# The last four heads' values by products of 512 columns, and one more gate behind the last head's attention

## The chip, the core and the metric

The kernel runs on one core of a Trainium2 chip. The metric is device time in microseconds of one execution. Before the change three executions took 2167.63 to 2169.94 us, median 2169.21.

## What is computed

One layer of a hybrid decoder trunk on 512 tokens of width 2048, in float32: a root-mean-square norm, an input projection, three kinds of mixers side by side, an output projection added to the input, and a squared-ReLU MLP. The change touches the projections of two of the mixers.

```python
h = rmsnorm(x, norm1_w)
proj = h @ w_in
sb_q, sb_k, sb_v, sc_b, sc_c, sc_h, gdn_qkv, gdn_z, gdn_a, gdn_b = jnp.split(proj, cuts, axis=-1)
y_sb = stick_breaking_attention(heads(sb_q), heads(sb_k), heads(sb_v))      # 6 heads of 128
y_sc = sc_b * causal_depthwise_conv(sc_c * sc_h, sc_conv_w)                 # 4 groups of 128
y_gdn = gdn_mixer(gdn_qkv, gdn_z, gdn_a, gdn_b, ...)                        # 6 heads, ends with * silu(gdn_z)
x = x + jnp.concatenate([y_sb, y_sc, y_gdn], axis=-1) @ w_out
```

In the stick-breaking attention the weights of a row come from the scores by a softplus, a cumulative sum along the keys and an exponential. sb_v has six heads of 128 columns. The delta-rule mixer (gdn) multiplies its normed output with silu(gdn_z), head by head; that is the gate.

## The kernel before

Products are made as three products of numbers split into a high part (fp32r) and the remainder: `mm3` (L114 to L118) multiplies high with high (L116), high with low (L117) and low with high (L118). All of them run on TensorE (PE). The activations of the layer's input are split once and kept for the whole mixer part: `xw`, 16 tiles `big` of 128 inputs by 512 tokens. Weights are read as needed by `wload` (L97): a DMA of 128 x 512 into `raw` on SyncE's queue (SP), a cast into `whi` on ScalarE (ACT, L103) and a subtraction into `wlo` on VectorE (DVE, L104). Each of `raw`, `whi` and `wlo` has four buffers. `gemm` (L129) makes one product of 128 output columns for all 512 tokens out of four such loads: 16 input tiles times three matmuls, 48 in all, with the weights as the stationary side and 512 tokens moving. It accumulates in a PSUM tile `mm`, of which there are three (MMB).

The mixers are called in the order of the calls L665 to L713, but a scheduler of the language orders the instructions of each engine, by the order of the program, by raised priorities (`base` and `scan` have 2000, weight loads 400) and by its own idea of when each is ready. The order on each engine is then fixed in the program: each engine runs its list strictly one after the other and waits where an operand is not ready.

The delta-rule heads come first. `gdn_scan` (L496) goes through four blocks of 128 tokens in steps, each a few small matmuls with an operation of ACT or DVE between them: L507, the bias on DVE (L509), L512, a copy on ACT (L514), L517, the state on DVE (L522), and the output (L526, L530, L532, L533). Behind the last block follow a square on ACT (L537), a sum on DVE (L539), a reciprocal root on ACT (L146, L148), a scaling on DVE (L541), four transposes on PE (L544) and a copy on ACT (L546). `gdn_gate(h)` (L549) is one `gemm` and a silu, and multiplies the head's output. `sc_group` (L561) makes three such products for one group of the short convolution; its third product stays in its `mm` tile until the convolution has been made on DVE (L573 to L576).

When the last scan is done, its memory is handed to the attention's pool `sbp` (L696). `sb_qk(h)` (L590) makes a head's query and key by `gemm` and splits them (`sb_split`, L580). `sb_attn(h)` (L593) makes the scores `z` on PE, then a chain on DVE and ACT (L608 to L625, with a cumulative sum L622), transposes the weights on PE (L633), splits them (L637, L638) and multiplies them with the values (L646 to L650).

The values of heads 0 and 1 are made at the kernel's start and come back by `v_load`. Those of heads 2 and 3 and of 4 and 5 are made by `v_stage(1)` and `v_stage(2)` (L269): for each of 16 input tiles and each of four blocks of 128 tokens three matmuls (L279, L280, L281) with the tokens as the stationary side and 256 columns of the weight moving, into the four halves of two `mm` tiles. One weight load of 512 columns holds two input tiles. `v_evac` (L231) scales and splits them into `vhl` (with a plain copy of the last block in `v3`).

Behind the attention the output projection starts: `gemm(wo[m], yh)`, where `yh` are the mixers' outputs, split at L733 and L734 and taken in the order `ORDER`, whose last entries are delta-rule head 3, attention head 4, delta-rule head 4, attention head 5 and delta-rule head 5.

Of the kernel before, what the change touches and what calls it, by code (L numbers as in the profile page):

```python
# [11 lines left out]
F32 = mybir.dt.float32  # L12
F32R = mybir.dt.float32r
AF = mybir.ActivationFunctionType
ALU = mybir.AluOpType

P = 128
T = 512
NB = T // P
D = 2048  # L20
KT = D // P
# [33 lines left out]
def trunk(ctx, tc, xT, wv1, wv2, wa, wo, wu, wd, vec, wf, out, dbg=None):  # L55
    nc = tc.nc
    V, S, G, PE = nc.vector, nc.scalar, nc.gpsimd, nc.tensor
# [15 lines left out]
    def mmps():  # L73
        pool, bufs = pool_of_mm
        return pool.tile([P, 512], F32, name="mm", tag="mm", bufs=bufs)

    def xps(tag):
        pool, bufs = pool_of[tag]
        return pool.tile([P, 512], F32, name=tag, tag=tag, bufs=bufs)
# [8 lines left out]
    def tmp(n=512):  # L88
        return per.tile([P, n], F32, name="tmp", tag="tmp", bufs=4)
# [7 lines left out]
    def wload(src, n, prio=None):  # L97
        with tc.high_priority(WPRIO if prio is None else prio):
            raw = per.tile([P, 512], F32, name="raw", tag="raw", bufs=4)
            nc.sync.dma_start(out=raw[:, :n], in_=src)  # L100
            hi = per.tile([P, 512], F32R, name="whi", tag="whi", bufs=4, align_bytes=256)
            lo = per.tile([P, 512], F32R, name="wlo", tag="wlo", bufs=4, align_bytes=256)
            S.copy(out=hi[:, :n], in_=raw[:, :n])  # L103
            V.tensor_tensor(out=lo[:, :n], in0=raw[:, :n], in1=hi[:, :n].bitcast(F32), op=ALU.subtract)  # L104
        return hi, lo
# [23 lines left out]
    def gemm(src, acts):  # L129
        p = mmps()  # L130
        for c in range(KT // CHUNK_KT):
            gemm_chunk(p, src, acts, c)
        return p

    def silu(x, s):

        S.activation(out=s, in_=x, func=AF.Abs)
        S.activation(out=s, in_=s, func=AF.Exp, scale=-1.0)
        S.activation(out=s, in_=s, func=AF.Ln, bias=1.0)
        V.scalar_tensor_tensor(out=s, in0=x, scalar=0.0, in1=s, op0=ALU.min, op1=ALU.subtract)  # L140
        S.activation(out=s, in_=s, func=AF.Exp)
        V.tensor_tensor(out=x, in0=x, in1=s, op=ALU.mult)
# [27 lines left out]
    def pt(shape, name, tag=None, bufs=1, dt=F32):  # L170
        return ph_pool.tile(shape, dt, name=name, tag=tag or name, bufs=bufs)
# [14 lines left out]
    xw = []  # L186
# [7 lines left out]
    for k in range(KT):  # L194
        hi, lo = wload(wv1[:, k, :], 268, 0)
# [6 lines left out]
                               op0=ALU.mult, op1=ALU.subtract)  # L202
        for b in range(NB):
            s = slice(b * P, (b + 1) * P)
# [15 lines left out]
    p = xps("r")  # L220
    PE.matmul(p, lhsT=ones, rhs=acc, start=True, stop=True)
    rsqrt_exp(R, p, 1.0 / D, None)
    rtok = pt([P, NB], "rtok")
    p = xps("r")
# [3 lines left out]
    rtoks = pt([P, NB], "rtoks")  # L228
    S.mul(out=rtoks, in_=rtok, mul=SCALE)

    def v_evac(src_of_blk, pool):  # L231

        hl = pool.tile([P, 2, NB, 256], F32R, name="vhl", bufs=2)
        v3 = pool.tile([P, 256], F32, name="v3", bufs=2)
        for b in range(NB):
            src = src_of_blk(b)
            S.activation(out=hl[:, 0, b], in_=src, func=AF.Copy, scale=rtok[:, b:b + 1])
            V.scalar_tensor_tensor(out=hl[:, 1, b], in0=src, scalar=rtok[:, b:b + 1],
                                   in1=hl[:, 0, b].bitcast(F32), op0=ALU.mult, op1=ALU.subtract)
            if b == NB - 1:  # L240
                S.activation(out=v3, in_=src, func=AF.Copy, scale=rtok[:, b:b + 1])
        return hl, v3

    vt = [None] * 3
    ab = pt([P, NB, 12], "ab")
# [3 lines left out]
    for c in range(2):  # L249
        t = tmp()  # L250
        for b in (2 * c, 2 * c + 1):
            S.activation(out=t[:, (b % 2) * 256:(b % 2) * 256 + 256], in_=v1p[b][:, :256], func=AF.Copy,
                         scale=rtok[:, b:b + 1])
        nc.sync.dma_start(out=vd[:, 2 * c:2 * c + 2].rearrange("p b f -> p (b f)"), in_=t)

    def v_load():
        hl = sp_pool.tile([P, 2, NB, 256], F32R, name="vhl", bufs=2)
        v3 = sp_pool.tile([P, 256], F32, name="v3", bufs=2)
        for c in range(2):
            t = tmp()  # L260
            nc.sync.dma_start(out=t, in_=vd[:, 2 * c:2 * c + 2].rearrange("p b f -> p (b f)"))
            o = hl[:, :, 2 * c:2 * c + 2].rearrange("p w b f -> p w (b f)")
            S.copy(out=o[:, 0], in_=t)
            V.tensor_tensor(out=o[:, 1], in0=t, in1=o[:, 0].bitcast(F32), op=ALU.subtract)
            if c == 1:
                S.copy(out=v3, in_=t[:, 256:512])
        vt[0] = (hl, v3)

    def v_stage(i):  # L269
        pp = [mmps(), mmps()]  # L270
        for c in range(0, KT, 2):
            hi, lo = wload(wv2[i - 1][:, c:c + 2, :].rearrange("p k f -> p (k f)"), 512)
            for kk in range(2):
                k = c + kk
                ws = slice(kk * 256, kk * 256 + 256)
                for b in range(NB):
                    s = slice(b * P, (b + 1) * P)
                    o = pp[b // 2][:, (b % 2) * 256:(b % 2) * 256 + 256]
                    PE.matmul(o, lhsT=xw[k][:, 0, s], rhs=hi[:, ws], start=k == 0 and b % 2 == 0, stop=False)  # L279
                    PE.matmul(o, lhsT=xw[k][:, 0, s], rhs=lo[:, ws], start=False, stop=False)  # L280
                    PE.matmul(o, lhsT=xw[k][:, 1, s], rhs=hi[:, ws], start=False, stop=k == KT - 1 and b % 2 == 1)  # L281
        vt[i] = v_evac(lambda b: pp[b // 2][:, (b % 2) * 256:(b % 2) * 256 + 256], sp_pool)

    ys = [None] * KT

# [29 lines left out]
    p = xps("r")  # L315
# [233 lines left out]
    def gdn_gate(h):  # L549
        p = gemm(wa[18 + h], xw)  # L550
        z = tmp()
        V.tensor_tensor(out=z, in0=p, in1=R, op=ALU.mult)
        silu(z, tmp())
        y = ys[10 + h]
        V.tensor_tensor(out=y, in0=y, in1=z, op=ALU.mult)
# [24 lines left out]
    def sb_split(p, name):  # L580
        hl = sp_pool.tile([P, 2, 512], F32R, name=name, tag=name, bufs=2)
        S.copy(out=hl[:, 0], in_=p)
        V.tensor_tensor(out=hl[:, 1], in0=p, in1=hl[:, 0].bitcast(F32), op=ALU.subtract)
        l0 = sp_pool.tile([P, P], F32, name=name + "0", tag=name + "0", bufs=2)
        S.copy(out=l0, in_=p[:, 0:P])
        return hl, l0

# [2 lines left out]
    def sb_qk(h):  # L590
        qk[h] = sb_split(gemm(wa[24 + 2 * h], xw), "sq") + sb_split(gemm(wa[24 + 2 * h + 1], xw), "sk")
# [93 lines left out]
    base(5)  # L685
    gdn_gate(3)
    sc_group(1)
    gdn_gate(4)
    sc_group(2)
    sc_group(3)  # L690
    scan(5)
# [5 lines left out]
    sp_pool = sbp.__enter__()  # L697
    sb_qk(0)
    v_load()
    sb_attn(0)  # L700
    sb_qk(1)
    sb_attn(1)
    v_stage(1)
    sb_qk(2)
    sb_attn(2)
    sb_qk(3)
    sb_attn(3)
    sb_qk(4)
    v_stage(2)
    sb_attn(4)  # L710
    sb_qk(5)
    sb_attn(5)
    gdn_gate(5)  # L713
    sbp.__exit__(None, None, None)
    pps.__exit__(None, None, None)
# [69 lines left out]
    for m in range(KT):  # L785
# [5 lines left out]
        p = gemm(wo[m], yh)  # L791
# [13 lines left out]
        i = m // 2  # L805
# [384 lines left out]
def layout(x, norm1_w, w_in, sc_conv_w, gdn_conv_w, gdn_a_log, gdn_dt_bias, gdn_norm_w,  # L1190
           w_out, norm2_w, w_up, w_down, final_norm_w):
    win = w_in[0]
    kc = lambda a: np.ascontiguousarray(a)
    cols = []
    for h in range(NH):
        cols += [3840 + 768 + h * P, 3840 + h * P, 3840 + 1536 + h * P]
    cols += [6144 + h * P for h in range(NH)]
    for h in range(NH):
        cols += [h * P, 768 + h * P]
    for g in range(NG):  # L1200
        cols += [2816 + g * P, 3328 + g * P, 2304 + g * P]
    wt = _ktile(win)
    wa = kc(np.stack([wt[:, :, c:c + P] for c in cols]))
    wv1 = kc(np.concatenate([wt[:, :, 1536:1792], wt[:, :, 6912:6924]], axis=2))
    wv2 = kc(np.stack([wt[:, :, 1792:2048], wt[:, :, 2048:2304]]))
    wo = _ktile(w_out[0]).reshape(P, KT, KT, P)[:, ORDER]
    wo = kc(wo.transpose(2, 0, 1, 3))


    wu = _ktile(w_up[0]).reshape(P, KT // 2, 2, FF // P // 2, 2, P)  # L1210
    wu = kc(wu.transpose(3, 2, 4, 0, 1, 5).reshape(FF // P // 2, 2, 2, P, KT // 2 * P))


    wd = _ktile(w_down[0]).reshape(P, FF // P // (2 * HK), HK, 2, 2, 2, 512)
    wd = kc(wd.transpose(1, 5, 3, 4, 0, 2, 6).reshape(FF // P // (2 * HK), 2, 2, 2, P, HK * 512))
    wf = kc(np.broadcast_to(final_norm_w[None, :], (P, D)))
    pcol = lambda v: v.reshape(-1, P).T
    rep = lambda v: np.broadcast_to(v[None, :], (P, v.shape[0]))
    scw = sc_conv_w[0].reshape(3, NG, P).transpose(2, 1, 0).reshape(P, 12)
    gcw = gdn_conv_w[0].reshape(4, 18, P).transpose(2, 1, 0).reshape(P, 72)  # L1220
    vec = kc(np.concatenate([
        pcol(norm1_w[0]), pcol(norm2_w[0]), scw, gcw,
        rep(gdn_a_log[0]), rep(gdn_dt_bias[0]), gdn_norm_w[0].reshape(P, 1)], axis=1))
    xT = kc(_ktile(x[0].T))
    return dict(xT=xT, wv1=wv1, wv2=wv2, wa=wa, wo=wo, wu=wu, wd=wd, vec=vec, wf=wf)
# [14 lines left out]
```

## Time and profile before

| | before |
|---|---|
| median of three executions | 2169.21 us |
| profiled execution, time | 2168.58 us |
| its span, first to last instruction | 2166.8 us |
| mean granted TensorE clock | 0.996 |
| PE / DVE / ACT busy | 99% / 77% / 49% |
| DMA queue of SP (q1) | 302.93 MB, 41.0% of 16 engines |
| first and last start of L279 | 542.0 and 670.3 us |

The page gives busy time by engine, the chain of work that ended last, and groups of equal instructions with their number, busy time, mean duration, and the idle time of the engine just before them. A timeline row gives the start, the duration, the engine, the line, the operation, what it writes and reads, and its size; `x3` is three equal instructions in one row, and the bracket is the engine's idle time before it and what ended it. A row of a window gives its length, then busy time and number of instructions of PE, the weight loads, DVE, ACT and POOL, then the granted clock, the DMA share and the rate. Matmuls overlap: a matmul's own duration is longer than the distance to the next one. The attention part lies between about 515 and 745 us.

### The profile page before, as it was taken

The page shows a single profiled execution, that of the slowest core. Times are in us where ns is not written, and L with a number is a line of the kernel's source. Part 1 is how long each engine was busy: PE and PEld are TensorE (multiplying, and loading weights), DVE is VectorE, ACT ScalarE, POOL GpSimd, SP SyncE. Part 2 cuts the span into 40 slices and gives each one's busy share as a digit, 9 for nine tenths or more (in the row PEclk, how much of TensorE's full clock was granted, in tenths as well). Part 3 has the DMA queues.
Part 4 walks back from the last instruction along what each step waited for, and adds up shares of the span by engine and source line. Part 5 has one row for each costly group of instructions (what it writes and reads, how often), then busy time and mean ns, then how long its engine had stood idle before and what let it go on. Part 6 is the DMA issues. An engine that isn't in the chain of part 4 may idle for free.

```text
span 2166.8 us, 33109 instructions
## 1 busy us (share of the span) xinstructions
PE 2136.6 (99%) x12674; PEld 1881.7 (87%) x12674; DVE 1660.4 (77%) x2360; ACT 1072.0 (49%) x1629; POOL 132.1 (6%) x188
## 2 busy tenths in 40 slices
PE   9999999999999999899999999999999999999998
PEld 8887888888988888699999999999888888888886
DVE  6678978644657755487888788778898898898897
ACT  5646666333445544344544454444554444454455
POOL 0000000000000011100000000000001000000101
PEclk9999999999999999999999999999999999999999
DMA  5333233322222354666656665666897877787774
GB/s 186 106 102 94 81 91 92 92 92 84 83 83 83 104 167 150 213 193 196 194 174 187 195 191 169 195 195 180 277 320 181 243 217 198 208 227 225 184 214 117
DMA packets 160719, 356.42 MB, mean 164 GB/s; under 512 B 20273, under 2 KB 62257, under 8 KB 160433
## 3 DMA queue, kind: packets, MB, share of 16 engines
q1 hardware_dynamic: 146304, 302.93, 41.0%
q0 software_dynamic: 13968, 50.86, 13.8%
q8 instruction: 99, 1.62, 0.3%
q14 instruction: 60, 0.48, 0.1%
q10 hardware_dynamic: 288, 0.52, 0.1%
HBM read 308.90 MB, written 45.36 MB: 163 GB/s over the span
## 4 chain that ended last, share of the span: by engine, by line
PE 95%; DMA 2%; DVE 1%; ACT 1%; issue 0%; SPq 0%; DVEq 0%; ACTq 0%
PE mm L117 11%; PE mm L116 11%; PE mm L118 11%; PE pu L118 10%; PE pu L116 10%; PE pu L117 10%; PE pp L117 9%; PE pp L118 9%; PE pp L116 9%; PE mm L280 1%; PE mm L281 1%; PE mm L279 1%; DMA q<-in_wu_dram 1%; DMA xq<-xs 1%; PE i L404 1%
## 5 line engine op out<-in xcount | busy, mean ns | idle before, releaser
L840 ACT CAST W<-q 128x1024 fp32r<-128x1024 f32 x446 | 465.6, 1051 | 581.4 <-PE pp L118 264.5
L841 DVE TENSOR_TENSOR W<-q,W 128x1024 fp32r<-128x1024 f32 x446 | 541.2, 1222 | 133.3 <-ACT W L840 129.3
L116 PE MATMUL mm<-big,whi 128*128 128x512 f32 x1024 | 404.7, 396 | 1.8 <-ACT whi L103 1.2
L117 PE MATMUL mm<-big,whi 128*128 128x512 f32 x1024 | 403.8, 394 | 0.0
L118 PE MATMUL mm<-big,wlo 128*128 128x512 f32 x1024 | 402.5, 393 | 0.0
L117 PE MATMUL pp<-W,A 128*128 128x512 f32 x888 | 345.7, 389 | 1.0 <-DVE W L841 1.0
L118 PE MATMUL pp<-W,A 128*128 128x512 f32 x888 | 345.6, 389 | 0.4 <-DVE A L841 0.4
L116 PE MATMUL pp<-W,A 128*128 128x512 f32 x888 | 342.9, 389 | 1.0 <-ACT W L840 1.0
L104 DVE TENSOR_TENSOR wlo<-raw,whi 128x512 fp32r<-128x512 f32 (+1 forms) x292 | 196.8, 676 | 159.2 <-ACT whi L103 151.4
L103 ACT CAST whi<-raw 128x512 fp32r<-128x512 f32 (+1 forms) x292 | 176.9, 607 | 277.3 <-PE mm L117 239.7
L116 PE MATMUL pu<-XS,W 128*128 128x256 f32 x1024 | 288.2, 281 | 9.5 <-ACT W L840 9.3
L118 PE MATMUL pu<-XS,W 128*128 128x256 f32 x1024 | 287.4, 281 | 0.5 <-DVE W L841 0.5
L117 PE MATMUL pu<-XS,W 128*128 128x256 f32 x1024 | 287.5, 281 | 0.0
L116 PEld LDWEIGHTS mm<-big,whi 128*128 128x128 f32 x1024 | 192.4, 188 | 41.2 <-ACT whi L103 1.8
L117 PEld LDWEIGHTS mm<-big,whi 128*128 128x128 f32 x1024 | 192.5, 188 | 39.1 <-DVE big L734 0.3
L118 PEld LDWEIGHTS mm<-big,wlo 128*128 128x128 f32 x1024 | 192.4, 188 | 39.0
L116 PEld LDWEIGHTS pu<-XS,W 128*128 128x128 f32 x1024 | 193.6, 189 | 10.2 <-ACT W L840 9.8
L116 PEld LDWEIGHTS pp<-W,A 128*128 128x128 f32 x888 | 166.7, 188 | 36.3 <-ACT W L840 1.8
L117 PEld LDWEIGHTS pp<-W,A 128*128 128x128 f32 x888 | 166.7, 188 | 36.2 <-DVE W L841 1.7
L118 PEld LDWEIGHTS pp<-W,A 128*128 128x128 f32 x888 | 166.7, 188 | 35.4 <-DVE A L841 0.8
L858 DVE TENSOR_TENSOR q<-q 128x1024 f32<-128x1024 f32 x159 | 194.2, 1222 | 1.4
L118 PEld LDWEIGHTS pu<-XS,W 128*128 128x128 f32 x1024 | 193.4, 189 | 0.8 <-DVE W L841 0.8
(302 smaller groups left out, 3278.3 us busy)
## 6 DMA issues: line engine op xcount, KB each, us to landing
q<-in_wu_dram SPq DMA_DIRECT2D x128, 512.0 KB, 4.4
q<-in_wd_dram SPq DMA_DIRECT2D x128, 512.0 KB, 5.6
raw<-in_wa_dram SPq DMA_DIRECT2D x192, 256.0 KB, 2.9
hs<-h SPq DMA_DIRECT2D x32, 1024.0 KB, 5.5
q<-in_wd_dram POOLq DMA_DIRECT2D x64, 512.0 KB, 7.3
ha<-hs SPq DMA_DIRECT2D x55, 512.0 KB, 6.5
q<-in_wu_dram POOLq DMA_DIRECT2D x33, 512.0 KB, 5.5
raw<-in_wo_dram SPq DMA_DIRECT2D x64, 256.0 KB, 3.0
```

The costliest lines, as they stand in the source:

```text
L103: S.copy(out=hi[:, :n], in_=raw[:, :n])
L104: V.tensor_tensor(out=lo[:, :n], in0=raw[:, :n], in1=hi[:, :n].bitcast(F32), op=ALU.subtract)
L116: PE.matmul(p, lhsT=lh, rhs=rh, start=first, stop=False, skip_group_check=more)
L117: PE.matmul(p, lhsT=lh, rhs=rl, start=False, stop=False, skip_group_check=more)
L118: return PE.matmul(p, lhsT=ll, rhs=rh, start=False, stop=last, skip_group_check=more)
L279: PE.matmul(o, lhsT=xw[k][:, 0, s], rhs=hi[:, ws], start=k == 0 and b % 2 == 0, stop=False)
L280: PE.matmul(o, lhsT=xw[k][:, 0, s], rhs=lo[:, ws], start=False, stop=False)
L281: PE.matmul(o, lhsT=xw[k][:, 1, s], rhs=hi[:, ws], start=False, stop=k == KT - 1 and b % 2 == 1)
L404: PE.matmul(pv[:, b], lhsT=kq[:, 2 * c + b, 0], rhs=kq[:, 2 * c + b], start=True, stop=True)
L840: return (S.copy(out=o[:, 0], in_=src), V.tensor_tensor(out=o[:, 1], in0=src, in1=o[:, 0].bitcast(F32), op=ALU.subtract))
L841: V.tensor_tensor(out=o[:, 1], in0=src, in1=o[:, 0].bitcast(F32), op=ALU.subtract))
L858: on_v = lambda t, u: V.tensor_tensor(out=t, in0=t, in1=u, op=ALU.add)
```

## The change

The values of heads 2 to 5 are made together, in two halves of the tokens. `v_half(half)` takes two blocks of 128 tokens, reads for each of 16 input tiles one weight tile of 512 columns (the four heads' columns), and makes for each block one `mm3` of 512 columns into an `mm` tile of its own. Each weight is read once per half, so twice. `v_half(0)` is called ahead of `sb_attn(1)`, `v_half(1)` ahead of `sb_attn(2)`; `v_stage(1)` stood between `sb_attn(1)` and `sb_qk(2)`, `v_stage(2)` ahead of `sb_attn(4)`. `vhl` has three buffers instead of two, the plain copies `sq0` and `sk0` one instead of two. `gdn_gate(4)` moves from between two groups of the short convolution to behind `sb_attn(5)`, ahead of `gdn_gate(5)`. The host lays the weight out as one array of 512 columns.

```diff
-    def v_evac(src_of_blk, pool):
-
-        hl = pool.tile([P, 2, NB, 256], F32R, name="vhl", bufs=2)
-        v3 = pool.tile([P, 256], F32, name="v3", bufs=2)
-        for b in range(NB):
-            src = src_of_blk(b)
-            S.activation(out=hl[:, 0, b], in_=src, func=AF.Copy, scale=rtok[:, b:b + 1])
-            V.scalar_tensor_tensor(out=hl[:, 1, b], in0=src, scalar=rtok[:, b:b + 1],
-                                   in1=hl[:, 0, b].bitcast(F32), op0=ALU.mult, op1=ALU.subtract)
-            if b == NB - 1:
-                S.activation(out=v3, in_=src, func=AF.Copy, scale=rtok[:, b:b + 1])
-        return hl, v3
+    def v_block(b, src, hl, v3):
+
+        S.activation(out=hl[:, 0, b], in_=src, func=AF.Copy, scale=rtok[:, b:b + 1])
+        V.scalar_tensor_tensor(out=hl[:, 1, b], in0=src, scalar=rtok[:, b:b + 1],
+                               in1=hl[:, 0, b].bitcast(F32), op0=ALU.mult, op1=ALU.subtract)
+        if b == NB - 1:
+            S.activation(out=v3, in_=src, func=AF.Copy, scale=rtok[:, b:b + 1])
...
-        hl = sp_pool.tile([P, 2, NB, 256], F32R, name="vhl", bufs=2)
+        hl = sp_pool.tile([P, 2, NB, 256], F32R, name="vhl", bufs=3)
...
-    def v_stage(i):
+    def v_half(half):
+
         pp = [mmps(), mmps()]
-        for c in range(0, KT, 2):
-            hi, lo = wload(wv2[i - 1][:, c:c + 2, :].rearrange("p k f -> p (k f)"), 512)
-            for kk in range(2):
-                k = c + kk
-                ws = slice(kk * 256, kk * 256 + 256)
-                for b in range(NB):
-                    s = slice(b * P, (b + 1) * P)
-                    o = pp[b // 2][:, (b % 2) * 256:(b % 2) * 256 + 256]
-                    PE.matmul(o, lhsT=xw[k][:, 0, s], rhs=hi[:, ws], start=k == 0 and b % 2 == 0, stop=False)
-                    PE.matmul(o, lhsT=xw[k][:, 0, s], rhs=lo[:, ws], start=False, stop=False)
-                    PE.matmul(o, lhsT=xw[k][:, 1, s], rhs=hi[:, ws], start=False, stop=k == KT - 1 and b % 2 == 1)
-        vt[i] = v_evac(lambda b: pp[b // 2][:, (b % 2) * 256:(b % 2) * 256 + 256], sp_pool)
+        for k in range(KT):
+            hi, lo = wload(wv2[:, k], 512)
+            for i in range(2):
+                b = 2 * half + i
+                s = slice(b * P, (b + 1) * P)
+                mm3(pp[i], xw[k][:, 0, s], xw[k][:, 1, s], hi, lo, k == 0, k == KT - 1)
+        for i in range(2):
+            if half == 0:
+                vt[1 + i] = (sp_pool.tile([P, 2, NB, 256], F32R, name="vhl", bufs=3), None)
+            else:
+                vt[1 + i] = (vt[1 + i][0], sp_pool.tile([P, 256], F32, name="v3", bufs=2))
+            for j in range(2):
+                v_block(2 * half + j, pp[j][:, i * 256:i * 256 + 256], *vt[1 + i])
...
-        l0 = sp_pool.tile([P, P], F32, name=name + "0", tag=name + "0", bufs=2)
+        l0 = sp_pool.tile([P, P], F32, name=name + "0", tag=name + "0", bufs=1)
...
     gdn_gate(3)
     sc_group(1)
-    gdn_gate(4)
     sc_group(2)
     sc_group(3)
     scan(5)
...
     sb_attn(0)
     sb_qk(1)
+    v_half(0)
     sb_attn(1)
-    v_stage(1)
     sb_qk(2)
+    v_half(1)
     sb_attn(2)
     sb_qk(3)
     sb_attn(3)
     sb_qk(4)
-    v_stage(2)
     sb_attn(4)
     sb_qk(5)
     sb_attn(5)
+    gdn_gate(4)
     gdn_gate(5)
...
-    wv2 = kc(np.stack([wt[:, :, 1792:2048], wt[:, :, 2048:2304]]))
+    wv2 = kc(wt[:, :, 1792:2304])
```

## The prediction

> **What bounds the kernel now.** I read the page first, for the engines' busy time and the chain that ended last.
>
> ```profile
> PE 2136.6 (99%) x12674; PEld 1881.7 (87%) x12674; DVE 1660.4 (77%) x2360; ACT 1072.0 (49%) x1629; POOL 132.1 (6%) x188
> ...
> PE 95%; DMA 2%; DVE 1%; ACT 1%; issue 0%; SPq 0%; DVEq 0%; ACTq 0%
> ```
>
> TensorE (PE) is busy 99% of the span and makes 95% of the chain. A change can gain only by taking work from PE, and it loses wherever it opens a wait there. So I went to PE's timeline, for what a product costs from start to start (a matmul's own 0.28 or 0.39 us overlaps the next), and to the group of L279 for the number.
>
> ```profile
> L279 PE MATMUL mm<-whi,big 128*128 128x256 f32 x128 | 36.2, 283 | 0.0
> ```
>
> ```profile
> 565.22 0.28 PE L279 MATMUL mm<-whi,big 128*128 128x256 f32 x1
> ...
> 569.53 0.28 PE L279 MATMUL mm<-whi,big 128*128 128x256 f32 x1
> ...
> 570.36 0.39 PE L118 MATMUL mm<-big,wlo 128*128 128x512 f32 x1
> ...
> 586.01 0.39 PE L118 MATMUL mm<-big,wlo 128*128 128x512 f32 x1
> ```
>
> Between the first two rows lie 36 products of 256 columns, between the last two 69 of 512. That is 4.31 / 36 = 0.1197 us and 15.65 / 69 = 0.2268 us each. PE waits for nothing there.
>
> The third thing read is the one place in the attention part where PE does wait: the end of the last delta-rule scan (L530 to L546) and head 0's scores (z). First PE, then ScalarE (ACT), then VectorE (DVE).
>
> ```profile
> 517.45 0.38 PE L526 MATMUL o<-vn,y 128*128 128x128 f32 x2
> 517.67 0.39 PE L530 MATMUL o<-Sn,kq 128*128 128x128 f32 x2
> ...
> 526.11 0.60 PE L544 MATMUL o<-ident,MT 128*128 128x128 f32 x4
> 526.46 0.47 PE L116 MATMUL mm<-big,whi 128*128 128x512 f32 x1
> ...
> 528.44 0.79 PE L116 MATMUL z<-sk,sq 128*128 128x512 f32 x3 [0.35 <-ACT sk L582]
> ...
> 530.33 0.28 PE L118 MATMUL z<-sk,sq 128*128 128x256 f32 x1
> 530.96 0.50 PE L116 MATMUL mm<-big,whi 128*128 128x512 f32 x1 [0.36 <-ACT sq L585]
> ```
>
> ```profile
> 518.09 0.27 ACT L532 COPY oi<-o 128x128 f32<-128x128 f32 x1 [1.42 <-PE o L530]
> 518.78 0.63 ACT L537 ACTIVATE MT<-y 128x512 f32<-128x512 f32 x1 [0.42 <-DVE y L533]
> ...
> 520.16 0.30 ACT L146 ACTIVATE ss<-ss,eps_c 128x4 f32<-128x4 f32 x1 [0.25 <-DVE ss L539]
> ...
> 526.74 0.69 ACT L546 ACTIVATE y<-o,vc 128x512 f32<-128x512 f32 x1 [1.41 <-PE o L544]
> ...
> 527.79 0.60 ACT L582 CAST sk<-mm 128x512 fp32r<-128x512 f32 x1
> ...
> 529.62 0.64 ACT L103 CAST whi<-raw 128x512 fp32r<-128x512 f32 x1
> 530.14 0.60 ACT L582 CAST sq<-mm 128x512 fp32r<-128x512 f32 x1
> 530.62 0.29 ACT L585 COPY sq<-mm 128x128 f32<-128x128 f32 x1
> ```
>
> ```profile
> 518.39 0.35 DVE L533 SCALAR_TENSOR_TENSOR y<-o,posg,oi 128x128 f32<-128x128 f32 x1 [0.99 <-ACT oi L532]
> 519.44 0.69 DVE L539 TENSOR_REDUCE ss<-MT 128x4 f32<-128x512 f32 x1 [0.70 <-ACT MT L537]
> ...
> 520.73 0.69 DVE L541 TENSOR_TENSOR MT<-y,ss 128x512 f32<-128x512 f32 x1
> ```
>
> After L530 the scan's tail runs on ACT and DVE alone until 521.42. The transposes (L544) could start then, and the attention's tiles are free only when L546 has read them. Meanwhile PE works through 42 products of head 1's query. Of the 13.51 us from 517.45 to 530.96, PE's work is 0.44 (L526, L530) + 42 x 0.2268 = 9.53 + 0.35 (L544) + about 1.6 (nine score products, three each of 512, 384 and 256 columns) = 11.9; some 1.6 us are idle.
>
> **The products.** 384 products of 256 columns become 192 of 512: 192 x (2 x 0.1197 - 0.2268) = **2.4 us less**, all on PE, which sets the end. Nothing hides any of it. The Trainium skill (TensorE: Matmul & The Clock Gate, Back-to-back issue gap) gives N / 2.4 + 2.5 ns for a warm product; by that estimate the gain would be 192 x 2.5 ns = 0.5 us. The trace's rows, 13 ns per pair, decide.
>
> **The gate that leaves the scan.** gate(4)'s 48 products (10.9 us) cost the same anywhere, but they stood beside the last scan. On PE, before, the end of that scan:
>
> ```order
> L118 MATMUL mm<-big,wlo 128x512
> L526 MATMUL o<-vn,y 128x128
> L530 MATMUL o<-Sn,kq 128x128
> L116 MATMUL mm<-big,whi 128x512
> ...
> L118 MATMUL mm<-big,wlo 128x512
> L544 MATMUL o<-ident,MT 128x128 x4
> L116 MATMUL mm<-big,whi 128x512
> ```
>
> The same place of the changed kernel (its lines are three lower here):
>
> ```order
> L118 MATMUL mm<-big,wlo 128x512
> L523 MATMUL o<-vn,y 128x128
> L527 MATMUL o<-Sn,kq 128x128
> L541 MATMUL o<-ident,MT 128x128 x4
> L116 MATMUL z<-sk,sq 128x512
> ```
>
> The 36 and 6 products of head 1's query have moved ahead of the scan's last step; nothing stands between it, the transposes and the scores. Head 1's key product cannot step in: its accumulator is one of three, which head 0's query, head 0's key and head 1's query hold until the attention's tiles are free. Worked out with the rows above, from L530's start: the tail ends at 521.42 - 517.67 = 3.75, and about 0.3 later because a weight split (0.69 on DVE) now stands ahead of its L533. PE is idle from 0.22 to 4.1 (3.9), transposes for 0.35, then waits the rest of 528.44 - 526.11 = 2.33 (2.0 idle). From the scores to the key product 2.52 pass, less the cast that no longer stands between (530.14 - 529.62 = 0.52); with 1.6 of work that leaves 0.4. Idle 6.3 against 1.6: **4.7 us more** (3.9 to 5.5).
>
> **The clock.** Such a pause touches the granted clock: in these stretches, the number behind POOL's busy time and its count.
>
> ```profile
> 902.80:906.21 3.41, 0.00 (x0) 0.00 (x0) 0.00 (x0) 0.00 (x0) 1.94 (x2) 1.00 1.01 308
> ...
> 909.63:913.04 3.41, 1.10 (x3) 0.81 (x4) 1.59 (x2) 2.57 (x4) 0.00 (x0) 0.50 1.05 247
> 913.04:916.45 3.41, 3.41 (x17) 3.41 (x17) 2.63 (x5) 1.13 (x2) 0.00 (x0) 0.50 1.08 406
> ...
> 2155.49:2158.90 3.41, 0.87 (x4) 0.38 (x2) 3.36 (x10) 2.75 (x11) 2.32 (x2) 1.00 0.27 102
> 2158.90:2162.31 3.41, 0.00 (x0) 0.00 (x0) 2.04 (x6) 1.58 (x3) 0.00 (x0) 0.50 0.64 243
> ```
>
> The clock falls to 0.50 at 906.21 and at 2158.90, both on one grid of 3.41 us, after a stretch with 0 and with 0.87 us of PE work; 1.10 did not lift it, a full stretch did. From L527's end to the scores lie about 6.1 us with 0.6 of matmul rows in them, so a stretch under 0.87 nearly always fits. The clock then falls 3.7 to 7 us after L527 and comes back one or two stretches later, after 2 to 5.5 us of work at half speed: **1.8 us more** (0 to 2.8). The Trainium skill (same page, Part 1: The HAM clock gate) has the clock halve after an idle window of about 3.4 us on a free-running grid; the grid agrees. If only a wholly idle window counted, 3.9 us would seldom hold one; the 0.87 row says that a little work doesn't save it.
>
> **Inside the scans.** A second place on PE, the step of scan(4) beside the short-conv products. Before, and then after:
>
> ```order
> L507 MATMUL s_4055<-Sn_4047,kq_3151 128x128
> L118 MATMUL mm_4757<-big_594,wlo_4815 128x512
> ...
> L116 MATMUL mm_4831<-big_278,whi_4852 128x512
> L512 MATMUL s_4059<-bp_4057,MT_3371 128x128
> L117 MATMUL mm_4831<-big_278,whi_4852 128x512
> ```
>
> ```order
> L117 MATMUL mm_4748<-big_672,whi_4805 128x512
> L504 MATMUL s_4055<-Sn_4047,kq_3151 128x128
> L118 MATMUL mm_4748<-big_672,wlo_4806 128x512
> L509 MATMUL s_4059<-bp_4057,MT_3371 128x128
> L116 MATMUL mm_4823<-big_122,whi_4826 128x512
> ```
>
> 23 products stood between the step and its answer, now one; and mm_4823 must wait until DVE has read mm_4748, since two accumulators still hold third products of short-conv groups. The two DVE operations behind it:
>
> ```profile
> 454.04 0.34 DVE L509 SCALAR_TENSOR_TENSOR bp<-s,negeg,y 128x128 f32<-128x128 f32 x1
> ...
> 468.27 0.68 DVE L564 TENSOR_TENSOR tmp<-mm,R 128x512 f32<-128x512 f32 x1
> ```
>
> 0.38 for L504 to end + 0.34 + 0.68 less 0.67 of PE work in between, and some hand-over: **0.8 us more** (0 to 1.4).
>
> **The loads.** Each half reads 16 weight tiles where a stage read 8, so 16 more DMAs on SP's queue, casts and splits, and a load is used up in 6 x 0.2268 = 1.36 us (before 24 x 0.1197 = 2.87).
>
> ```profile
> raw<-in_wa_dram SPq DMA_DIRECT2D x192, 256.0 KB, 2.9
> ```
>
> ```profile
> L104 DVE TENSOR_TENSOR wlo<-raw,whi 128x512 fp32r<-128x512 f32 x65 | 44.8, 689 | 44.5 <-ACT whi L103 42.2 <-PE z L633 1.8
> ```
>
> ```profile
> 547.26 2.96 DVE L622 TENSOR_TENSOR_SCAN e<-ones,sp 128x511 f32<-128x511 f32 x4
> 550.13 0.67 DVE L104 TENSOR_TENSOR wlo<-raw,whi 128x512 fp32r<-128x512 f32 x1
> 550.72 1.49 DVE L624 TENSOR_TENSOR zs<-zs,e 128x1280 f32<-128x1280 f32 x1
> ```
>
> A load's round is 2.9 + 0.6 + 0.69 = 4.2 us over four buffers, 1.05 each: SP and ACT keep up while DVE is clear. DVE isn't: in the first half head 0's chain runs there. On DVE after, in the first half:
>
> ```order
> L104 TENSOR_TENSOR wlo<-raw,whi 128x512
> L619 SCALAR_TENSOR_TENSOR e<-ones,sp 128x511
> L619 SCALAR_TENSOR_TENSOR e<-ones,sp 128x383
> L619 SCALAR_TENSOR_TENSOR e<-ones,sp 128x127
> L619 SCALAR_TENSOR_TENSOR e<-ones,sp 128x255
> L104 TENSOR_TENSOR wlo<-raw,whi 128x512
> ```
>
> The cumulative sums (2.96) stand between the fifth split and the sixth. Four buffers give 4.1 us from a release to the use, 1.3 of it for cast and split: 2.8 of slack, and the sums come behind L618 and a key split. I put the sixth split some 0.8 us late: **0.8 us more** (0 to 2.5). Behind the second half's attention the heavy part is done; nothing there.
>
> **The end.** gate(4)'s loads, activation chain and product go ahead of the last head's chain on ACT and DVE, where the first three output products cover them. After the last head's value product four products stand where eight did: 4 x 0.2268 less the cast (0.52) that no longer precedes its split, **0.3 us more** (0 to 0.9). The other regroupings (evacuation, buffers of vhl, sq0) issue as many operations; nothing.
>
> **The sum.** -2.4 + 4.7 + 1.8 + 0.8 + 0.8 + 0.3 = +6.0 on the profiled execution's 2168.58: 2174.6. That execution lies 0.63 under the median of the three, 2169.21, so **2175.2**. A measurement of this kernel can tell about 0.2%, 4.3 us.
>
> **The rivals.** *The clock holds* (0.22): the four transposes break the pause, so that the 1.8 goes. It decides at the 0.87 row: if transposes count for more than that row's products, no stretch is idle. Then 2173.4, not slower by 0.2%. For it: no row shows a pause broken by transposes. Against: 0.6 is less than 0.87. *Starved halves* (0.12): each long DVE operation ahead of a split delays PE, in both halves, by 2.5 more: 2177.7. Against: DVE's idle 44.5 us ahead of L104 today. *The products gain nothing* (0.08): with the weights as the moving side the pair costs what it did: 2177.6. Against: L279 already moves the weights. That leaves my forecast 0.58. To be faster by 0.2% the change would need 4.3 us, where the products give 2.4 and the whole idle above 1.6: 0.03.
>
> My forecast's own spread (1.6 us) leaves a seventh of it within 0.2%; with most of the first rival that makes same 0.28, slower 0.69. The range takes the first rival with small waits (2171) to the starved one with the upper clock bound (2179).
>
> **What would show it.** Right: PE idle about 4 us ahead of the transposes and 2 ahead of head 0's scores, the granted clock at 0.5 there, starts 0.227 apart in the halves. Wrong: a gap under 3 us there, key products between transposes and scores, or a wait for wlo over 3 us in total in the first half.

## The result, and the profile after

The changed kernel takes **2177.10 us** (median of 6, 2175.96 to 2178.76), the kernel before 2168.94 (median of 6, 2167.63 to 2169.94): ratio 1.0039, 95% interval 1.0028 to 1.0050. It is slower by 8.2 us, 2 more than forecast and inside the range. (Ratios here are worked out from the runs with their interval, and can differ from the quotient of two medians in the fourth decimal.) The profiled execution took 2177.24, its span is 2175.5.

The page after: busy times, then the chain.

```profile
PE 2136.7 (98%) x12482; PEld 1873.8 (86%) x12482; DVE 1670.6 (77%) x2376; ACT 1082.3 (50%) x1645; POOL 133.7 (6%) x188
...
PE 92%; DVE 3%; DMA 2%; ACT 1%; issue 1%; SPq 0%; POOL 0%; DVEq 0%; ACTq 0%; POOLq 0%
```

PE has 192 products fewer, and its share of the chain fell from 95% to 92%: DVE (1% to 3%) and issue (0% to 1%) took it over. VectorE now stands on the path for longer. PE's timeline shows where, at the end of scan(5):

```profile
516.45 0.39 PE L527 MATMUL o<-Sn,kq 128*128 128x128 f32 x2
520.53 1.11 PE L541 MATMUL o<-ident,MT 128*128 128x128 f32 x4 [3.69 <-DVE MT L538]
523.38 1.33 PE L116 MATMUL z<-sk,sq 128*128 128x512 f32 x3 [1.74 <-ACT sk L579]
...
526.21 0.41 PE L118 MATMUL z<-sk,sq 128*128 128x256 f32 x1
526.43 0.58 PE L116 MATMUL mm<-big,whi 128*128 128x512 f32 x1
```

PE has nothing to do between L527 and the transposes (bracket 3.69), and again ahead of head 0's scores (1.74). The score products are longer than in the kernel before (256 columns take 0.41 us against 0.28), which is the clock. The windows, on the clock's own grid (the clock is the number behind POOL's busy time and count):

```profile
516.59:520.00 3.41, 0.25 (x3) 0.05 (x1) 1.86 (x4) 1.62 (x5) 0.00 (x0) 1.00 0.36 105
520.00:523.42 3.42, 1.15 (x5) 0.75 (x5) 1.02 (x2) 1.74 (x4) 0.00 (x0) 0.50 0.00 0
523.42:526.83 3.41, 3.41 (x10) 3.05 (x11) 3.41 (x7) 2.08 (x6) 0.13 (x1) 0.50 0.00 0
526.83:530.24 3.41, 3.41 (x16) 2.82 (x15) 0.97 (x3) 0.62 (x1) 0.75 (x3) 1.00 0.00 0
```

After a stretch with 0.25 us of PE work the clock is halved for two stretches.

To split the 8.7 us between the two profiled executions I cut each at three rows of PE's timeline: the first gemm product, the first transposes that leave the attention part, the last product. Before, and then after:

```profile
14.16 0.50 PE L116 MATMUL mm<-big,whi 128*128 128x512 f32 x1 [0.58 <-ACT whi L103]
...
746.11 0.66 PE L774 MATMUL t<-ident,x 128*128 128x128 f32 x4
...
2155.97 0.39 PE L118 MATMUL mm<-W,A 128*128 128x512 f32 x1
```

```profile
13.59 0.50 PE L116 MATMUL mm<-big,whi 128*128 128x512 f32 x1 [0.36 <-ACT whi L103]
...
751.01 0.66 PE L771 MATMUL t<-ident,x 128*128 128x128 f32 x4
...
2163.99 0.39 PE L118 MATMUL mm<-W,A 128*128 128x512 f32 x1
```

The part with scans and attention ("the mixers" below) takes 731.95 before and 737.42 after, **+5.5**. The rest up to the last product, mostly the MLP, takes 1409.86 and 1412.98, **+3.1**. The program's end behind it takes 2166.8 - 2155.97 = 10.8 and 2175.5 - 2163.99 = 11.5, **+0.7**. The first product started 0.57 earlier, which is a matter of the execution: it lies between 13.1 and 14.2 us in all the traces here. So the forecast's +6.0 is in the mixers, and 3.8 us came from a part of the program that the edit doesn't touch.

### The profile page after: what moved, and what is told of

Its sections match the earlier page's. It is cut to its first block, busy times and chain, and to the rows that moved or that the text cites. A ratio compares the mean times of both kernels' runs of the same rounds, so it can differ in the third digit from the quotient of the medians.

```text
span 2175.5 us, 32814 instructions
## 1 busy us (share of the span) xinstructions
PE 2136.7 (98%) x12482; PEld 1873.8 (86%) x12482; DVE 1670.6 (77%) x2376; ACT 1082.3 (50%) x1645; POOL 133.7 (6%) x188
## 4 chain that ended last, share of the span: by engine, by line
PE 92%; DVE 3%; DMA 2%; ACT 1%; issue 1%; SPq 0%; POOL 0%; DVEq 0%; ACTq 0%; POOLq 0%
PE mm L116 11%; PE mm L117 11%; PE mm L118 11%; PE pu L118 10%; PE pu L116 10%; PE pu L117 10%; PE pp L117 9%; PE pp L118 9%; PE pp L116 9%; DMA q<-in_wu_dram 1%; DMA xq<-xs 1%; PE i L401 0%; DVE W L838 0%; PE t L771 0%; PE z L630 0%
## 5 line engine op out<-in xcount | busy, mean ns | idle before, releaser
L103 ACT CAST whi<-raw 128x512 fp32r<-128x512 f32 (+1 forms) x308 | 187.3, 609 | 290.3 <-PE mm L117 257.5
L104 DVE TENSOR_TENSOR wlo<-raw,whi 128x512 fp32r<-128x512 f32 (+1 forms) x308 | 207.3, 676 | 153.3 <-ACT whi L103 146.9
L116 PEld LDWEIGHTS pu<-XS,W 128*128 128x128 f32 x1024 | 193.6, 189 | 11.9 <-ACT W L837 11.5
```

The source lines that it names most:

```text
L116: PE.matmul(p, lhsT=lh, rhs=rh, start=first, stop=False, skip_group_check=more)
```

## The experiments

All were timed in five rounds. Times of different chips are compared through the kernel before, which ran beside each: its medians were 2168.55 with the first four, 2168.15 with the next four, 2168.48 with the next two and 2168.05 with the last.

**1. The gate alone.** The kernel before, with gate(4) moved:

```
     sc_group(1)
-    gdn_gate(4)
     sc_group(2)
...
     sb_attn(5)
+    gdn_gate(4)
     gdn_gate(5)
```

> The kernel before with one thing changed: the gate of head 4 is made behind the last attention head; the values stay as they were. Theory A (the stall where the last scan hands over to the attention is the price, and the move of the gate alone makes it): PE idle of about 3.9 us ahead of the transposes and 2.0 ahead of head 0's scores, the clock at 0.50 behind it, +6.3 in the attention part against before by the rows of the two traces, +0.9 in the scan step beside the short convolution, +0.4 at the end; 2176.5. Theory B (the further 3 us that the trace of after shows in the MLP come from nine products that the scheduler put elsewhere there, which it does in this kernel too): 2176.5 + 2.7 = 2179.2. Rival C (the halves' loads are the price, the gate is free): 2169.

Measured: 2177.07 us, +8.5, ratio 1.0041 (1.0028 to 1.0055). PE's timeline in it:

```profile
515.84 0.39 PE L530 MATMUL o<-Sn,kq 128*128 128x128 f32 x2
519.92 0.66 PE L544 MATMUL o<-ident,MT 128*128 128x128 f32 x4 [3.69 <-DVE MT L541]
522.32 1.33 PE L116 MATMUL z<-sk,sq 128*128 128x512 f32 x3 [1.74 <-ACT sk L582]
```

The same two idle times with none of the halves: the stall belongs to the gate's move. This trace has one loss more that the changed kernel's traces don't have: in the MLP, behind a wait of 2.0 us at 1567.16, the clock was halved for one stretch (1568.55 to 1571.96).

**2. The halves alone.** The changed kernel, with gate(4) back at its old place:

```
     sc_group(1)
+    gdn_gate(4)
     sc_group(2)
...
     sb_attn(5)
-    gdn_gate(4)
     gdn_gate(5)
```

> The changed kernel with one thing put back: the gate of head 4 stands beside the last scan again, and the values are made by halves. Theory A: no stall, -2.4 for the products and +0.2 for the first half's loads; 2166.7. Theory B (the MLP's order, which differs from before here too, costs 2.7): 2169.4. Rival C (the halves' loads are the price): 2175 or more.

Measured: 2175.22 us, +6.7, ratio 1.0035 (1.0023 to 1.0048). The stall at the scan's end is gone, as expected, but not the time: here my theory fell. PE's timeline at the last head:

```profile
734.94 0.39 PE L118 MATMUL mm<-big,wlo 128*128 128x512 f32 x1
738.77 2.40 PE L630 MATMUL z<-ident,zs 128*128 128x128 f32 x10 [3.44 <-ACT zs L622]
740.82 0.78 PE L643 MATMUL o<-hl,vhl 128*128 128x512 f32 x1
...
745.86 0.97 PE L116 MATMUL mm<-big,whi 128*128 128x512 f32 x3 [1.32 <-ACT big L730]
```

```profile
734.20:737.60 3.40, 1.13 (x5) 0.59 (x4) 3.15 (x5) 0.36 (x2) 0.00 (x0) 1.00 0.21 67
737.60:741.00 3.40, 2.23 (x11) 2.23 (x11) 0.46 (x1) 1.93 (x3) 0.00 (x0) 0.51 0.30 108
741.00:744.40 3.40, 3.40 (x12) 2.84 (x11) 1.25 (x3) 0.90 (x3) 0.00 (x0) 0.50 0.00 0
```

In the kernel before, the last value stage (192 products of 256 columns) ran until 670.7 us, beside head 3's chain, and 81 products of 512 columns were left to stand beside the last head's chain (713.41 to 731.63). With the halves all value products are over by then, and only 54 products stand there (722.84 to 734.94): PE waits 3.6 us ahead of the last head's transposes (738.77 - 734.94 - 0.23), 1.3 ahead of the output products, and the clock is halved for two stretches. In the changed kernel, with gate(4) behind the last head, 85 products stand there. So the 48 products of gate(4) cover either the end of the last scan or the end of the last head; whichever is bare costs about the same.

**3. Work for the idle clock.** The changed kernel, with 30 transposes of the identity between L527 and scan(5)'s transposes, into a tile that nobody reads:

```
...
+        if h == 5:
+            warm = xps("b")
+            with behind(last):
+                for _ in range(30):
+                    after = [PE.transpose(warm[:, :P], ident, ident)]
         po = xps("o")
...
```

> The changed kernel with 30 transposes of a constant added on PE between the last scan's final product and its transposes; nobody reads what they write. They take about 3.3 us of a pause of 3.9. Theory A (the pause makes the clock fall, which costs 1.8 beyond the idle time itself): the clock stays at 1.00, head 0's scores run 0.22 apart, and the time is 1.8 below the changed kernel: 2175.3. Rival (what the slow products lose is hidden behind ScalarE's and VectorE's casts, which set the pace there): the clock stays up and the time is as in the changed kernel, 2177.1.

Measured: 2174.25 us, +5.7, ratio 1.0032 (1.0019 to 1.0044). Its windows:

```profile
517.63:521.04 3.41, 2.96 (x26) 2.48 (x23) 1.38 (x2) 1.14 (x3) 0.00 (x0) 1.00 0.27 77
521.04:524.45 3.41, 1.66 (x7) 1.25 (x8) 2.20 (x4) 3.40 (x8) 0.00 (x0) 1.00 0.00 0
524.45:527.86 3.41, 3.41 (x11) 2.83 (x10) 2.46 (x5) 0.42 (x3) 0.88 (x3) 0.50 0.00 0
```

The first pause no longer halves the clock; the second one does, after a stretch with 1.66 us of PE work in it. The mixers take 736.99, only 0.4 us less than after (0.7 less than in experiment 5). What the median gained beyond that can't be put to this place.

**4. Cover from head 1.** The changed kernel, with the split query and key of the even heads in the pool of the `y` tiles, one buffer each, and the odd heads' where all were, one buffer each; the plain copies `sq0` and `sk0` of all heads move to the `y` pool too. The attention's own pool takes over the scan's space and is not free until the scan's tail has been read; the `y` pool is free earlier. Head 0's query and key can so be split, and their accumulators given back, while scan(5) still runs:

```
...
-        hl = sp_pool.tile([P, 2, 512], F32R, name=name, tag=name, bufs=2)
+        even = name in ('sq', 'sk') and h % 2 == 0
+        hl = (y_pool if even else sp_pool).tile([P, 2, 512], F32R, name=name, tag=name, bufs=1 if name in ('sq', 'sk') else 2)
...
```

> The changed kernel, gate of head 4 still at the end, but the split query and key of the even heads lie in memory of their own, so that head 0's can be read out of their accumulators before the last scan is done and head 1's key product can run in the pause. Nothing else differs, but the MLP's order is again that of before. Theory A (the three held accumulators are why nothing covers the pause): 36 products stand between the scan's last product and its transposes, the idle time falls under 1 us, the clock stays up; 2177.1 less 6.3 and the 1.6 that before lost there too is 2169.2. Theory B (and the MLP's 2.7 go with its order): 2166.5. Rival (the key product arrives late for want of weights, or the pause only moves): 2174 or more.

Measured: 2168.71 us, +0.2, ratio 1.0002 (0.9993 to 1.0011). PE's timeline:

```profile
517.17 0.39 PE L527 MATMUL o<-Sn,kq 128*128 128x128 f32 x2
517.31 0.48 PE L118 MATMUL mm<-big,wlo 128*128 128x512 f32 x1
...
525.38 0.39 PE L117 MATMUL mm<-big,whi 128*128 128x512 f32 x1
525.61 0.60 PE L541 MATMUL o<-ident,MT 128*128 128x128 f32 x4
525.96 0.47 PE L118 MATMUL mm<-big,wlo 128*128 128x512 f32 x1
...
529.71 0.39 PE L116 MATMUL z<-sk,sq 128*128 128x512 f32 x1
...
532.78 0.50 PE L116 MATMUL mm<-whi,big 128*128 128x512 f32 x1 [0.35 <-ACT sq L583]
```

36 products now stand between L527 and the transposes and 16 between them and the scores, 0.227 us apart, with no idle time. Head 0's key is split on ACT at 504.91, in the kernel after at 522.73. The mixers take 730.85, 6.6 us less than after. The stall was thus a matter of what PE was *allowed* to do: the products were there, and their accumulators were held.

**5. The changed kernel again**, to have it beside the next three.

> The changed kernel once more, beside the others on one chip. Its first trace was 3.1 us longer than before's behind the mixers: 1.7 at the start of the MLP (11.2 idle where before had 9.5), 0.7 at 944 us, 0.7 near 1564 us. If the first and the last are the spread of single executions, this trace has an idle of 9.2 to 9.6 at the MLP's start, as four others had, and the median lies at 2168.6 + 5.5 (mixers) + 0.7 (the wait at 944) = 2174.8. If they belong to the change, both are there again and the time is 2177.

Measured: 2175.61 us, +7.5, ratio 1.0034 (1.0022 to 1.0047). Mixers 737.68 (+5.7 on before), rest 1410.62 (+0.8), end 11.5 (+0.7). Of the first execution's +3.1 in the rest, 2.4 did not come again.

**6. Both pauses filled.** Experiment 3 with 16 more idle transposes behind scan(5)'s own:

```
...
+        if h == 5:
+            with behind(done):
+                for _ in range(16):
+                    PE.transpose(warm[:, :P], ident, ident)
```

> As the run with 30 idle-time transposes, and 16 more of them behind the last scan's own transposes, so that the second pause, before head 0's scores, is filled as well. Theory (pauses of either place make the clock fall): the clock stays at 1.00 from 515 to 530, the scores and the key's products run at 0.22 from the start, and the time is 1.8 below the changed kernel in this call. Rival (the clock fell in the run with 30 for another reason than the second pause, or the lost time is hidden): no gain.

Measured: 2173.66 us, +5.5, ratio 1.0025 (1.0015 to 1.0035), 1.95 under experiment 5 beside it. Windows:

```profile
519.81:523.22 3.41, 2.99 (x26) 2.52 (x24) 1.35 (x3) 1.94 (x5) 0.00 (x0) 1.00 0.01 3
523.22:526.63 3.41, 3.36 (x16) 2.66 (x17) 3.41 (x7) 1.96 (x6) 0.29 (x1) 1.00 0.00 0
```

The clock stays at 1.00. The transposes of scan(5) start 4.08 us behind L527, as in the kernel after; the 1.95 us (2.4 in the mixers) is the price of the halved clock. Experiment 3's median is nearly as low although its clock fell once; the medians don't resolve that step, the mixers' 736.99 there and 735.24 here do.

**7. Experiment 4 with head 2's query and key ahead of the first half:**

```
     sb_qk(1)
+    sb_qk(2)
     v_half(0)
     sb_attn(1)
-    sb_qk(2)
     v_half(1)
```

> The run with the even heads' query and key apart, and head 2's query and key called ahead of the first half of the values, which then starts later than head 0's cumulative sums. If the halves' loads are late only beside those sums (0.52 + 0.39 + 0.49 there), those 1.4 go and it takes 2167.3. Rival (they are as late beside head 1's chain): 2168.7, as that run, or more.

Measured: 2170.76 us, +2.6, ratio 1.0011 (1.0003 to 1.0020). The halves then meet head 1's chain on DVE in place of head 0's, and the end of the attention has less cover (PE waits 1.32 us ahead of the output products, in experiment 4 0.40): mixers 732.51, 1.7 more than experiment 4. The rival was right.

**8. The MLP's reordered products.** In the trace after, PE waits once inside the MLP where the kernel before doesn't:

```profile
944.35 0.28 PE L117 MATMUL pu<-XS,W 128*128 128x256 f32 x1
945.17 0.38 PE L118 MATMUL pu<-XS,W 128*128 128x256 f32 x1 [0.54 <-DVE W L838]
```

In the written order of the second pair of `up_pair`, 14 products of `XP` stand ahead of the products that free a weight tile, where 5 stood before: 9 x 0.1197 = 1.08 us later. This kernel holds them back:

```
...
+                if g == 1 and n == 1:
+                    mms(n, 0, 2)
+                    with behind(*held):
+                        last = mms(n, 2, KP)
+                else:
+                    last = mms(n, 0, KP)
+                if g == 0 and n == 4:
+                    held.append(last)
...
```

> The changed kernel with one order put back that the scheduler had changed on its own: in the MLP's second pair, the first product stops behind 6 matmuls until the last six of the pair before it are issued, as in the kernel before, where 11 stood ahead. Theory (the nine products put ahead there delay the release of a weight tile by 9 x 0.12 = 1.1 and cost 0.7): no wait at 944, and 0.7 less than the changed kernel in this call. Rival (that wait is the spread of executions): it is there again, and no gain.

Measured: 2176.39 us, +8.2, ratio 1.0038 (1.0025 to 1.0051); 0.8 above experiment 5, not below. The wait is gone from the trace: the 72 products among which it stood take 8.55 us from the first one's start to the start of the product behind them, in experiment 5 9.31. But the MLP's start lost about as much: behind its first wait PE ran 6.1 us at half clock (916.52 to 922.60), in experiment 5 4.2 (917.34 to 921.58), which at half speed is 0.9 us less work. So the trace gives the wait its price, some 0.8 us, and the time doesn't show its removal.

**9. The kernel before, with the buffers of 4 and the order of 8.**

> The kernel before, values and gate as they were, with the even heads' query and key apart, and with the MLP's second pair held to the order it has in before. If the held accumulators are also what leaves before its 1.6 us of idle time at the end of the last scan, those go: 2168.2 - 1.6 = 2166.6. Rival (the idle time comes from the casts' own pace): 2168.2.

Measured: 2167.06 us, -1.4, ratio 0.9995 (0.9986 to 1.0004): the lowest of all, and not told apart from before. PE's busy time at the scan's end, in this kernel and in the one before:

```profile
517.00:530.00 13.00, 13.00 (x62) 10.81 (x62) 6.73 (x11) 6.34 (x14) 0.00 (x0) 1.00 0.26 81
```

```profile
517.00:530.00 13.00, 12.60 (x59) 10.02 (x58) 6.17 (x11) 6.41 (x14) 0.00 (x0) 1.00 0.25 81
```

By the starts, the idle time of the prediction's 1.6 us falls to 0.2. The changed kernel with the same buffers (experiment 4) stands at +0.2: with this stall gone from both, the merged products show no gain in the time.

**10. Another gate for scan(4).** Experiments 4 and 8 together, with gate(3) moved to where gate(4) had been:

```
-    gdn_gate(3)
     sc_group(1)
+    gdn_gate(3)
     sc_group(2)
```

> The changed kernel with the even heads' query and key apart, the gate of head 3 called between two groups of the short convolution (where before had the gate of head 4), and the MLP's order held as in before. If the scan step that waits there (0.46 + 0.37) is a matter of what is called between those groups, 0.9 of the earlier run with query and key apart goes: 2167.5. Rival (another scan step loses its cover instead): 2168.5 or more.

Measured: 2170.03 us, +1.6, ratio 1.0009 (1.0000 to 1.0018); the profiled execution, 2167.18, was the fastest of its 11. At the step of scan(4) a wait of 0.7 us stays, and one step on a longer one comes up, 470.56 - 468.55 less 0.22 for the two products:

```profile
468.55 0.39 PE L504 MATMUL s<-Sn,kq 128*128 128x128 f32 x2
470.56 0.50 PE L116 MATMUL mm<-big,whi 128*128 128x512 f32 x1 [1.62 <-DVE tmp L565]
```

**11. The loads alone.** The kernel before, with each value weight tile of the last heads loaded and split a second time, into tiles that nobody reads:

```
             hi, lo = wload(wv2[i - 1][:, c:c + 2, :].rearrange("p k f -> p (k f)"), 512)
+            wload(wv2[i - 1][:, c:c + 2, :].rearrange("p k f -> p (k f)"), 512)
```

> The kernel before, in which each weight tile of the values is read, cast and split a second time into a tile that nobody uses: 16 more loads, as the halves have, and nothing else of the change. In every kernel with the halves the last output write landed 10.64 us after the last product's start instead of 9.97, because the third of the last writes on SP started 4.63 after it instead of 4.32. Theory (that comes with the 16 more loads, by their number alone): the same 4.63 and a span that ends 11.51 instead of 10.83 after the last product's start, nothing lost in the mixers, since a load's share of products is still 1.43 us with the copy: 2168.4 + 0.7 = 2169.1. Rival (the late write belongs to another part of the halves): 4.32 and 10.83 as before, 2168.4. Second rival (the loads themselves starve PE beside head 0's cumulative sums): 1 to 2 us lost between 540 and 570.

Measured: 2168.97 us, +0.9, ratio 1.0003 (0.9994 to 1.0012). The mixers take 732.12, 0.2 more than before. But the program ends as late behind its last product (2168.8 - 2157.27 = 11.5) as after does. The writes of the result on SP's queue in this kernel (the third starts 4.62 us after the last product's start):

```profile
2157.27 0.39 PE L118 MATMUL mm<-W,A 128*128 128x512 f32 x1
...
2161.89 0.33 SPq L1111 DMA_DIRECT2D out_dram<-xq  x1
```

Before, and then after:

```profile
2160.29 0.41 SPq L1110 DMA_DIRECT2D out_dram<-xq  x1
```

```profile
2168.62 0.33 SPq L1107 DMA_DIRECT2D out_dram<-xq  x1
```

That is 4.32 before and 4.63 after. The end of the span is 0.7 later in every kernel here with 16 more loads and in none without.

## Why the prediction was right, point by point

**The products: -2.4, right.** The value products of the second half, after:

```profile
598.97 0.39 PE L116 MATMUL mm<-whi,big 128*128 128x512 f32 x1
...
602.83 0.40 PE L118 MATMUL mm<-whi,big 128*128 128x512 f32 x1
```

17 starts in 3.86 us, 0.227 each: the third rival (no gain) is out. The Trainium skill (TensorE: Matmul & The Clock Gate, Back-to-back issue gap) gives 512 / 2.4 + 2.5 = 216 ns for an isolated warm product of 512 columns; the trace has 227 for these, and the trace decided.

**The pause at the scan's end: +4.7, right in place, cause and size.** From L527's start 516.45 the next product could have come 0.22 later; the transposes came at 520.53: 3.86, forecast 3.9. From them to the scores 2.85 passed, of which the transposes themselves take 0.70 at half clock (0.35 at full): 2.15, forecast 2.0. Behind the scores PE did not wait (forecast 0.4). Together that is 4.4 more than the 1.6 of the kernel before. That held accumulators are the cause, and not a lack of products, is shown by experiment 4.

**The clock: +1.8, right.** Two halved stretches, and 1.95 us between experiments 5 and 6. The first rival, that the four transposes save the clock, is out. What was wrong is the bound under it: I took 0.87 us as the most PE work that doesn't save a stretch. In experiment 3 a stretch with 1.66 didn't save it either.

**The step of scan(4): +0.8, right.** PE's timeline after:

```profile
454.56 0.38 PE L504 MATMUL s<-Sn,kq 128*128 128x128 f32 x2
454.69 0.48 PE L118 MATMUL mm<-big,wlo 128*128 128x512 f32 x1
455.38 0.49 PE L509 MATMUL s<-bp,MT 128*128 128x128 f32 x2 [0.21 <-DVE bp L506]
456.07 0.47 PE L116 MATMUL mm<-big,whi 128*128 128x512 f32 x1 [0.20 <-DVE tmp L561]
```

Product, answer and next product are 0.69 apart where 0.2 to 0.3 would do. Both waits are on the two DVE rows that the prediction named; by starts they come to 0.9.

**The loads: +0.8, too high.** PE's timeline after, in the first half:

```profile
544.56 0.61 PE L116 MATMUL mm<-whi,big 128*128 128x512 f32 x2
545.19 0.50 PE L117 MATMUL mm<-wlo,big 128*128 128x512 f32 x1
545.53 0.40 PE L118 MATMUL mm<-whi,big 128*128 128x512 f32 x1
```

0.63 for two products and 0.34 for one: 0.3 us over 0.227 each, and no more in that half. In experiment 4, where the half begins ahead of head 0's scores, the waits for loads at 547 and 550 us come to 0.9 us (the one at 532, 0.5, is ended by a plain copy on ACT, L583, not by a load), and in experiment 2 there is none. That this depends on how far head 0's chain has come on DVE is likely, but no run shows it alone. The starved rival's 2.5 was not reached in either half. The loads themselves cost PE nothing at 24 products each (experiment 11).

**The end of the attention: +0.3, right.** The output products start 0.56 late at 746.73; by the starts of the whole place it is 0.4 more than before.

**The mixers' sum: +6.0 forecast, +5.5 and +5.7 measured.** The terms held one by one, and the largest difference is the loads.

**What the sum lacked** is everything behind the mixers. I costed only the places where the edit moves work. Yet the order is written out by a scheduler over the whole program, and in the changed kernel nine products stand elsewhere 200 us later: +0.7 to 0.8 (the wait at 944.35, in experiments 1, 2, 3, 5 and 6 too, and in none of 4, 7, 8, 9, 10 and 11). The 72 products among which it stands take 9.1 to 9.3 us in the kernels with the wait and 8.45 to 8.55 in those without. And 16 more loads make the last writes later: +0.7, which experiment 11 shows with nothing else changed; by what mechanism a load of the attention part moves the last writes was not tried. Together 5.7 + 0.8 + 0.7 = 7.2, the difference of experiment 5's profile from before's (2175.74 - 2168.58). Most of the rest of the first execution's 3.1 lies at the start of the MLP, where PE waits for the first weights: 9.32 us before, 11.00 after, and 9.44 in experiment 5, which is the same kernel; another 0.6 lies in a wait at 1567 us (1.68 after, 1.13 in experiment 5). Since the same kernel shows both, that is a spread of executions, not the change.

**The gate and the halves are not two separate terms.** The prediction put the loss down to the gate's move alone. Experiment 1 bears that out against the kernel before, but experiment 2 shows that the halves without the move lose about as much: with the values made early, too few products are left beside the last head's chain, where gate(4) stands in the changed kernel. It is one loss, of some 7 us, that stands at either of two places.

## What to carry to other kernels

Before work is moved that costs the same anywhere, ask what serial chain it stands beside, and what else may run there: count the free accumulators and buffers, not the products that are left. A pause in TensorE has two prices, the wait and the halved clock behind it, and a buffer that lets another head's product go ahead (experiment 4) took back both. Where a scheduler writes the order of the whole program, compare the order far behind the edit and at the program's end too; in this case 1.5 of some 7 us came from there, by the traces.

## What the runs showed of the hardware that was not expected

The granted clock fell after stretches of the 3.41 us grid with 0.25 and with 1.66 us of PE work, and held after stretches with 2.96 and 2.99. The traces hold narrower cases. Here is a stretch of the kernel after, in the MLP, and the one behind it:

```profile
1564.49:1567.90 3.41, 1.73 (x8) 1.13 (x7) 3.41 (x4) 1.92 (x2) 0.00 (x0) 1.00 1.04 416
1567.90:1571.31 3.41, 3.41 (x16) 2.81 (x16) 3.41 (x5) 1.36 (x3) 0.86 (x1) 1.00 0.80 264
```

The clock held after 1.73, and so it did after 1.71 in experiment 6 (2159.20) and 1.79 in experiment 10 (468.91). The level thus lies near half a stretch, 1.7 us; one stretch with 1.54 in experiment 5 (515.40) held too, so the busy time of these rows is not exactly what counts. The Trainium skill (TensorE: Matmul & The Clock Gate, Part 1: The HAM clock gate) names an idle window as what halves the clock; the grid and the half rate agree with it, the 1.66 does not.

46 transposes that compute nothing made the kernel faster by 1.95 us, since they kept the clock at 1.00 through a pause of 6 us.
